# A hybrid decoder layer on one core: its tasks listed in another order, with engines and PSUM banks of copies and splits chosen anew

## The chip, the cores and the metric

One Trainium2 chip, of which one core is used. The time of an execution is the device time in microseconds (us). The number to predict is the median over runs of the changed kernel; that of the kernel before is 780.19 us (three runs: 783.53, 779.92 and 780.19).

## The reference

One decoder layer for 512 positions and 1024 channels in float32, batch 1. The core of it:

```python
mod = (silu(c) @ w_ada + b_ada)
sh1, sc1, gt1, sh2, sc2, gt2 = split(mod, 6)
h = rmsnorm(x, norm1_g) * (1 + sc1) + sh1
z = h @ w_in
zq, zkc, zvc, zks, zvs, zkw, zvw, zg, zs = split(z, cuts)
o_attn = nsa_attention(zq, zkc, zvc, zks, zvs, zkw, zvw, sigmoid(zg), pe_k, pe_v, w_ck1, w_ck2, w_cv1, w_cv2)
y_ssm = s5_mixer(zs, lam_re, lam_im, log_step, b_re, b_im, c_re, c_im, d_skip, w_glu, b_glu)
mix = concat([rmsnorm(o_attn, attn_norm_g), rmsnorm(y_ssm, ssm_norm_g)])
x = x + gt1 * (mix @ w_o)
h = rmsnorm(x, norm2_g) * (1 + sc2) + sh2
u = causal_dwconv(h @ w_up, conv_w, conv_b)
a, v = split(u, 2)
x = x + gt2 * ((silu(a) * v) @ w_down)
return rmsnorm(x, normf_g)
```

`nsa_attention` has 8 query heads and 2 key/value heads of 64, rotary positions on queries and keys, and three branches (compressed blocks of 32 keys, selected blocks, a window), each head's branches mixed by gates. `s5_mixer` is a diagonal state space model with 32 groups of 16 channels and 64 complex states, followed by GELU and a GLU.

## The kernel before, in words

**Matmuls.** Every large product is made of three float32 matmuls at the rounded precision fp32r: `split` (L107 to L109) makes of a float32 operand a high part (a cast, by `cpy`, L64 on ACT, L67 on DVE, L71 on POOL) and a low part (what the cast left over, a subtraction, L109, on DVE or POOL), and `mm3` (L119 to L123) adds high x high (L121), high x low (L122) and low x high (L123). `weights` (L111 to L117) does that for a weight tile: DMA from SP into one of four buffers tagged "raw", then cast and subtraction into one of four buffers tagged "unit". A tile is named by what it is for: `uinq0` to `uinq3` are the four tiles of the query columns of `w_in`, `uos0` to `uos3` and `uoa0` to `uoa3` those of `w_o` for the SSM half and the attention half, `uup` and `udn` those of the feed-forward loop; the raw buffer has `r` in place of `u`.

**Stages.** The first 120 us load x and the state space parameters, make the modulation from `w_ada`, the normalised and transposed h (`hh`, `hl`), the tables of the state space model, and the projections of keys and values. To 160 us POOL and DVE run the scan of the state X (`madd`, L689 to L692: a product pra, a sum ada, an addition to X), while PE computes the hidden layer of the compressed keys (hid, L747). `comp` takes that hidden layer through a GELU (copy to cg L67, then `gelu2`, L1242 to L1247, ACT and DVE in turn), transposes it (hT, L759) and multiplies it on (co, L763 and L772). Then the four query tiles zq0 to zq3 are projected, each over eight k-tiles, two of them in each of uinq0 to uinq3, and each is rotated by `rope` (L611 to L613 on DVE, L616) and transposed into QS (qx, L794 to L798). The powers of the model (VV, L348 and L349: two products, of which one lands in a temporary vw, and their sum) are made beside that. From 200 us on, the attention runs by query tile and pair of heads: scores (L834), masked maxima (L839 and L848), exponentials on ACT (L853), scaling by the gates (L64, L69 or L73), transposes p (L895), and products with the values (po, L901). Between them stand the SSM outputs y, their transposes yT (L1036), GELU (ys, ga), split (yh) and GLU (L1057), the sums for the norms (ssq, with `rsqrt` in L171 to L173: DVE, then a power on POOL), and the output projection: `residual` (L1081 to L1092) for the SSM half (os) and for the attention half (oa), where F (L908 on) makes mixa (L919) from the attention output. N0 to N3 normalise for the feed-forward layer (hx, L944 and L947, then a split to h2h and h2l), and eup computes the first columns of it with the two early weights eu. From 400 to 755 us the feed-forward loop runs 22 blocks of up and 22 of down weights, and the end normalises and stores.

**What sets the order.** Two tables in the source. `ORDER` lists 210 task names; each is called once in that order. `PICK` holds choices that differ from a default: for a copy or subtraction its engine (`e_...`, `h_...`: A, V or P), for a tile its PSUM bank group (`ps_...`: acc 3, tr 2, ms 2, pv 1) or its buffer. Both are looked up by `kn`. The calls are not the final order: the tile scheduler arranges the instructions of each engine by its own estimate of when they can start, with the order of the calls as a priority, and puts in the waits. So the table moves instructions also in places that it does not name.

Of the kernel before, what the change touches and what calls it, by code (L numbers as in the profile page):

```python
# [18 lines left out]
ORDER = """  # L19
ident c x0 xn0 x1 xn1 x2 xn2 x3 xn3 rows sp vt silu a0 p0 ws0 step a1 p1 z0 z1 ws1 z2 dT a2 p2 z3 ws2 pw bc a3 p3 z4 z5 ws3 ri bct0 bct1 z6  # L20
z7 Bb1 Bb2 W W1 W0 zu U0 U1 cst A4 X W3 KS mid wk1 wk2 wk0 U2 wk3 s2 L1 U3 wv0 W2 L2 wv2 zk1 L3 L0 g11 kx1 wv3 zk0 kx0 zk3 kx3 Ss b2 zk2 g13
VC wv1 zv1 chain g12 kx2 cw g10 zv0 zv2 VV b1 AM1 b0 AM0 VV3 zv3 hid0 hid1 hid2 hid3 comp wq0 wq3 wq1 wq2 zq0 qx0 zq1 zq3 qx3 zq2 qx2 VV5
qx1 M s3 VV0 s1 VV6 VV2 b3 VV1 K1 s0 S00 O00 XV K2 K0 K3 S01 O01 glu0 glu1 VV4 S02 O02 K4 K5 Y1 K6 Y0 S03 yh O03 VV7 K7 Y2 ys Y3 yT0 S10 yT1
O10 ge0 yT3 ge1 yT2 S11 ge3 ge2 gl3 S12 O11 xr gl1 gl0 gl2 gt1 O12 ssq wos R1 woa S13 O13 S20 O20 S21 O21 S22 O22 S23 S30 O23 R0 R3 R2 F1 F0
O30 S31 O31 S32 S33 O32 O33 cv F2 N0 N1 F3 N2 N3 eu0 eup0 eu1 eup1
# [4 lines left out]
def kn(name, *opts):  # L30
    if opts:
        SEEN.setdefault(name, opts)
    return PICK.get(name, opts[0] if opts else SEEN[name][0])
D = 1024
# [1276 lines left out]
```

## Time and profile before

| | us |
|---|---|
| runs (median of three) | 780.19 (779.92 to 783.53) |
| the profiled execution, its own time | 781.08 |
| its span, first to last instruction | 779.3 |
| PE busy | 713.8 (92% of the span) |
| DVE busy | 476.7 (61%) |
| POOL busy | 315.5 (40%) |
| ACT busy | 298.6 (38%) |
| mean granted TensorE clock | 0.972 |

PE is TensorE's matmuls, DVE VectorE, ACT ScalarE, POOL GpSimd, SP the queue that issues the transfers. A busy engine may be busy beside another one; only where PE waits does the work of the others show in the time.

### The profile page before, as it was taken

The page shows a single profiled execution, that of the slowest core. Times are in us where ns is not written, and L with a number is a line of the kernel's source. Part 1 is how long each engine was busy: PE and PEld are TensorE (multiplying, and loading weights), DVE is VectorE, ACT ScalarE, POOL GpSimd, SP SyncE. Part 2 cuts the span into 40 slices and gives each one's busy share as a digit, 9 for nine tenths or more (in the row PEclk, how much of TensorE's full clock was granted, in tenths as well). Part 3 has the DMA queues.
Part 4 walks back from the last instruction along what each step waited for, and adds up shares of the span by engine and source line. Part 5 has one row for each costly group of instructions (what it writes and reads, how often), then busy time and mean ns, then how long its engine had stood idle before and what let it go on. Part 6 is the DMA issues. An engine that isn't in the chain of part 4 may idle for free.

```text
span 779.3 us, 11258 instructions
## 1 busy us (share of the span) xinstructions
PE 713.8 (92%) x4171; PEld 570.3 (73%) x4171; DVE 476.7 (61%) x1011; ACT 298.6 (38%) x617; POOL 315.5 (40%) x312
## 2 busy tenths in 40 slices
PE   3998998878799898989889999999999999999993
PEld 2677787546677576768589888888888888888883
DVE  3369848369877786685775477465753554323337
ACT  7444325111476956255423333332333321212223
POOL 2589947897521525254531320310233113131023
PEclk9999999979989999999979999999999999999997
DMA  8666235752121017000052143343422333323102
GB/s 267 235 225 222 95 127 161 276 222 78 30 46 38 1 45 279 2 1 6 22 209 94 61 156 132 111 135 109 142 102 81 109 109 108 109 82 108 55 1 108
DMA packets 30843, 87.64 MB, mean 112 GB/s; under 512 B 4712, under 2 KB 9252, under 8 KB 30757
## 3 DMA queue, kind: packets, MB, share of 16 engines
q1 hardware_dynamic: 30789, 86.92, 32.9%
q8 instruction: 33, 0.54, 0.3%
q14 instruction: 21, 0.17, 0.1%
HBM read 82.71 MB, written 2.10 MB: 109 GB/s over the span
## 4 chain that ended last, share of the span: by engine, by line
PE 72%; DVE 9%; POOL 6%; DMA 6%; ACT 4%; issue 3%; SPq 0%; POOLq 0%; ACTq 0%; DVEq 0%
PE up L123 10%; PE up L121 10%; PE up L122 9%; PE dn L123 5%; PE dn L122 5%; PE dn L121 5%; PE po L901 2%; PE sc L834 2%; PE p L895 2%; DMA raws<-in_bc_dram 2%; POOL prl L689 1%; PE eup L121 1%; PE y L1015 1%; PE eup L122 1%; PE eup L123 1%
## 5 line engine op out<-in xcount | busy, mean ns | idle before, releaser
L123 PE MATMUL up<-h2h,uup 128*128 128x512 f32 x320 | 126.3, 395 | 0.0
L121 PE MATMUL up<-h2h,uup 128*128 128x512 f32 x320 | 126.3, 396 | 0.0
L122 PE MATMUL up<-h2l,uup 128*128 128x512 f32 x320 | 126.0, 394 | 0.0
L1178 DVE SCALAR_TENSOR_TENSOR us<-up,cst,us 128x511 f32<-128x511 f32 x80 | 59.8, 747 | 64.4 <-ACT us L1176 63.2
L1176 ACT ACTIVATE us<-up,cst 128x512 f32<-128x512 f32 x40 | 31.1, 778 | 105.9 <-PE up L123 105.8
L123 PEld LDWEIGHTS up<-h2h,uup 128*128 128x128 f32 x320 | 60.1, 188 | 14.2
L122 PEld LDWEIGHTS up<-h2l,uup 128*128 128x128 f32 x320 | 60.0, 188 | 14.1
L121 PEld LDWEIGHTS up<-h2h,uup 128*128 128x128 f32 x320 | 60.1, 188 | 13.9
L122 PE MATMUL dn<-udn,ghs 128*128 128x512 f32 x176 | 68.5, 389 | 0.0
L123 PE MATMUL dn<-udn,ghs 128*128 128x512 f32 x176 | 68.5, 389 | 0.0
L121 PE MATMUL dn<-udn,ghs 128*128 128x512 f32 x176 | 68.0, 389 | 0.0
L109 POOL TENSOR_TENSOR uup<-rup,uup 128x1024 fp32r<-128x1024 f32 x13 | 32.8, 2525 | 64.7 <-ACT uup L64 51.4
L109 DVE TENSOR_TENSOR uup<-rup,uup 128x1024 fp32r<-128x1024 f32 x27 | 37.1, 1375 | 14.8 <-ACT uup L64 14.7
L73 POOL TENSOR_SCALAR Ss<-Ss,sm 128x384 f32<-128x384 f32 (+3 forms) x38 | 23.2, 622 | 42.0 <-DVE sm L857 24.7
L109 POOL TENSOR_TENSOR udn<-rdn,udn 128x1024 fp32r<-128x1024 f32 x7 | 17.2, 2458 | 54.7 <-DVE udn L67 27.2
L121 PEld LDWEIGHTS dn<-udn,ghs 128*128 128x128 f32 x176 | 33.0, 188 | 6.9
L122 PEld LDWEIGHTS dn<-udn,ghs 128*128 128x128 f32 x176 | 33.0, 188 | 6.9
L123 PEld LDWEIGHTS dn<-udn,ghs 128*128 128x128 f32 x176 | 33.0, 188 | 6.8
L834 PE MATMUL sc<-KS,QS 128*128 128x288 f32 (+2 forms) x128 | 32.6, 355 | 3.5 <-DVE mp L848 1.7
L853 ACT ACTIVATE Ss<-Ss,mx 128x128 f32<-128x128 f32 (+3 forms) x64 | 35.1, 550 | 0.0
L64 ACT ACTIVATE uup<-rup 128x1024 fp32r<-128x1024 f32 x28 | 29.4, 1050 | 12.7 <-PE up L123 12.7
L109 DVE TENSOR_TENSOR udn<-rdn,udn 128x1024 fp32r<-128x1024 f32 x15 | 19.9, 1328 | 17.1 <-ACT udn L64 10.4
(450 smaller groups left out, 1729.6 us busy)
## 6 DMA issues: line engine op xcount, KB each, us to landing
rup<-in_w_up_dram SPq DMA_DIRECT2D x44, 512.0 KB, 3.4
rdn<-in_w_down_dram SPq DMA_DIRECT2D x22, 512.0 KB, 3.2
mid<-in_w_ada_dram SPq DMA_DIRECT2D x14, 512.0 KB, 4.0
adaa<-in_w_ada_dram SPq DMA_DIRECT2D x8, 512.0 KB, 6.1
adap<-in_w_ada_dram SPq DMA_DIRECT2D x8, 512.0 KB, 5.4
adag<-in_w_ada_dram SPq DMA_DIRECT2D x8, 512.0 KB
adab<-in_w_ada_dram SPq DMA_DIRECT2D x7, 512.0 KB, 3.5
xt<-in_x_dram SPq DMA_DIRECT2D x4, 512.0 KB, 5.4
```

The lines of the kernel that those rows point to most:

```text
L64: A.activation(dst, src, AF.Copy, **({} if s is None else {"scale": s}))
L73: P.tensor_scalar(dst, src, s, 1.0, op0=ALU.mult, op1=ALU.mult)
L109: eng.tensor_tensor(out=lo, in0=src, in1=f(hi), op=ALU.subtract)
L121: PE.matmul(ps, w[0], m[0], start=start, stop=False)
L122: PE.matmul(ps, w[0], m[1], start=False, stop=False)
L123: PE.matmul(ps, w[1], m[0], start=False, stop=stop)
L834: PE.matmul(ps[:, :n], v.QS[:, h, qs], v.KS[:, g, x, c0:c0 + n], start=x == 0, stop=x == 1)
L853: A.activation(Sv[:, br, :nk], Sv[:, br, :nk], AF.Exp, bias=mx[:, e, 1 + br:2 + br], scale=0.125, accum_out=sm[:, e, 1 + br:2 + br])
L895: PE.transpose(pc_[:, o:o + 128], v.Ss[:, ui, e, br, kc * 128:(kc + 1) * 128], ident)
L901: PE.matmul(half(e), VT[:, kc, br, g], pT[:, o:o + 128], start=kc == 0 and br == 0, stop=kc == qt > 0 and br == 1)
L1176: A.activation(u_, ps, AF.Identity, bias=cv[:, 3, c_:c_ + 1], scale=cv[:, 2, c_:c_ + 1])
L1178: V.scalar_tensor_tensor(u_[:, d:], ps[:, :S - d], cv[:, 2 - d, c_:c_ + 1], u_[:, d:], op0=ALU.mult, op1=ALU.add)
```

## The change

Only the two tables are edited; the 210 tasks, the 3519 matmuls and the arithmetic are the same. In `PICK` some 65 entries are added, dropped or changed: engines of about 50 copies and splits, the PSUM bank group of nine tiles, two buffers (mixa2 from raw to pt, pz101 to sw). Those that the prediction speaks of, one entry to a line:

```diff
-'h_inv3': 'V'
+'h_inv3': 'P'
...
+'e_os1': 'V'
...
-'h_oa3': 'V'
...
-'e_h23': 'V'
```

`e_os1` is the engine of the subtraction for uos1 (default POOL); `h_oa3` that of the cast for uoa3 (default ACT); `e_h23` that of the low part of the last tile of h2 (default POOL); `h_inv3` that of the cast of a tile of the value columns. About twenty of the other entries are casts and subtractions of uup, udn and gh in the feed-forward loop, of which most change between DVE and POOL, in both directions.

In `ORDER` about forty names stand elsewhere. Two of its lines, where the places below are:

```diff
-VC wv1 zv1 chain g12 kx2 cw g10 zv0 zv2 VV b1 AM1 b0 AM0 VV3 zv3 hid0 hid1 hid2 hid3 comp wq0 wq3 wq1 wq2 zq0 qx0 zq1 zq3 qx3 zq2 qx2 VV5
...
+g13 wv1 zv1 chain g12 kx2 cw g10 zv0 VV zv2 zv3 AM1 b1 b0 VV3 AM0 hid0 hid1 hid2 hid3 VC comp wq0 wq3 wq2 wq1 zq0 qx0 zq1 zq3 qx3 VV5 zq2
```

**First place: compressed keys and query weights (about 158 to 180 us).** On DVE, the GELU of the compressed keys among the scan's additions and the casts of the query weights. Before:

```order
L691 TENSOR_TENSOR ada3_1210<-pra3_1209 128x224
L692 TENSOR_TENSOR X_714<-X_714,ada3_1210 128x7x32
L67 COPY cg_1463<-hid_1414 128x256
L1244 TENSOR_SCALAR cg_1463<-cg_1463 128x256
L689 TENSOR_TENSOR pra5_1219<-A4_685,zu_661 128x448
L1245 TENSOR_TENSOR cg_1463<-cg_1463 128x256
L691 TENSOR_TENSOR ada5_1220<-pra5_1219 128x224
L692 TENSOR_TENSOR X_714<-X_714,ada5_1220 128x7x32
L67 CAST uinq0_1492<-rinq0_1490 128x1024
L1247 SCALAR_TENSOR_TENSOR cg_1463<-cg_1463 128x256
```

Now:

```order
L689 TENSOR_TENSOR pra3_1208<-A4_686,zu_622 128x448
L691 TENSOR_TENSOR ada3_1209<-pra3_1208 128x224
L67 COPY cg_1463<-hid_1413 128x256
L692 TENSOR_TENSOR X_715<-X_715,ada3_1209 128x7x32
L1244 TENSOR_SCALAR cg_1463<-cg_1463 128x256
L1245 TENSOR_TENSOR cg_1463<-cg_1463 128x256
L689 TENSOR_TENSOR pra5_1218<-A4_686,zu_622 128x448
L691 TENSOR_TENSOR ada5_1219<-pra5_1218 128x224
L1247 SCALAR_TENSOR_TENSOR cg_1463<-cg_1463 128x256
L67 CAST uinq0_1492<-rinq0_1490 128x1024
L692 TENSOR_TENSOR X_715<-X_715,ada5_1219 128x7x32
```

The last step of the GELU (L1247) stands ahead of the cast of uinq0 and of the second addition to X; the copy to cg stands ahead of the first. On POOL, the low halves of the four query weights among the last steps of the scan. Before:

```order
L109 TENSOR_TENSOR uinq0_1492<-rinq0_1490,uinq0_1492 128x1024
L691 TENSOR_TENSOR ada6_1225<-pra6_1224 128x224
L689 TENSOR_TENSOR pra7_1229<-A4_685,zu_661 128x448
L109 TENSOR_TENSOR uinq3_1497<-rinq3_1495,uinq3_1497 128x1024
L109 TENSOR_TENSOR uinq1_1502<-rinq1_1500,uinq1_1502 128x1024
L692 TENSOR_TENSOR X_714<-X_714,ada6_1225 128x7x32
L691 TENSOR_TENSOR ada7_1230<-pra7_1229 128x224
L109 TENSOR_TENSOR uinq2_1507<-rinq2_1505,uinq2_1507 128x1024
L692 TENSOR_TENSOR X_714<-X_714,ada7_1230 128x7x32
```

Now:

```order
L109 TENSOR_TENSOR uinq0_1492<-rinq0_1490,uinq0_1492 128x1024
L691 TENSOR_TENSOR ada6_1224<-pra6_1223 128x224
L689 TENSOR_TENSOR pra7_1228<-A4_686,zu_622 128x448
L109 TENSOR_TENSOR uinq3_1497<-rinq3_1495,uinq3_1497 128x1024
L109 TENSOR_TENSOR uinq2_1502<-rinq2_1500,uinq2_1502 128x1024
L692 TENSOR_TENSOR X_715<-X_715,ada6_1224 128x7x32
L109 TENSOR_TENSOR uinq1_1507<-rinq1_1505,uinq1_1507 128x1024
L691 TENSOR_TENSOR ada7_1229<-pra7_1228 128x224
L692 TENSOR_TENSOR X_715<-X_715,ada7_1229 128x7x32
```

uinq2 and uinq1 have changed places, and the sum ada7 is now behind the subtraction of uinq1. On PE the first three query tiles now use uinq0 one after the other, and all that is left of them needs uinq1 first. Further on, on DVE, one of the sums VV that stood ahead of the first rotary instruction (L611 of zq0) is behind it.

**Second place: the GLU among the scores (about 268 to 280 us).** On PE, the first matmuls of the GLU (their operands are the four tiles of yh) and the scores sc of the last units of query tile 2. Before:

```order
L834 MATMUL sc261_3055<-KS_736,QS_1510 128x512
L887 MATMUL pc201_2929<-ident_67,scz1_104 128x128
L895 MATMUL p2010_2933<-ident_67,Ss_1026 128x128
L834 MATMUL sc261_3055<-KS_736,QS_1510 128x512
L895 MATMUL p2010_2933<-ident_67,Ss_1026 128x128 x2
L834 MATMUL sc270_3065<-KS_736,QS_1510 128x288
L895 MATMUL p2010_2933<-ident_67,Ss_1026 128x128
L121 MATMUL glu3_2453<-yh_2184,uglu0_1983 128x512
L121 MATMUL glu1_2545<-yh_2184,uglu0_1983 128x512
L834 MATMUL sc270_3065<-KS_736,QS_1510 128x288
L122 MATMUL glu3_2453<-yh_2184,uglu0_1983 128x512
```

Now:

```order
L834 MATMUL sc250_2948<-KS_553,QS_1510 128x288 x2
L121 MATMUL glu0_2453<-yh_2184,uglu0_1972 128x512
L121 MATMUL glu3_2471<-yh_2184,uglu0_1972 128x512
L895 MATMUL p2002_2876<-ident_67,Ss_904 128x128 x4
L122 MATMUL glu0_2453<-yh_2184,uglu0_1972 128x512
L123 MATMUL glu0_2453<-yh_2184,uglu0_1972 128x512
L122 MATMUL glu3_2471<-yh_2184,uglu0_1972 128x512
L123 MATMUL glu3_2471<-yh_2184,uglu0_1972 128x512
L887 MATMUL pc200_2849<-ident_67,scz0_103 128x128
L834 MATMUL sc251_2954<-KS_553,QS_1510 128x512 x2
L834 MATMUL sc260_3049<-KS_553,QS_1510 128x288 x2
L834 MATMUL sc261_3055<-KS_553,QS_1510 128x512 x2
```

GLU tiles 0 and 3 begin ahead of sc251 to sc270; before, tiles 3 and 1 began behind sc251, sc260 and sc261 and among sc270. On DVE the first subtraction for yh is the 430th row of the engine instead of the 461st. sc271 and the scores of tile 3, which stood among the GLU matmuls, now stand behind most of them.

**Third place: the weights of the SSM half (about 300 to 310 us).** On POOL, the powers r_s of the norm and the subtractions of uos. Before:

```order
L173 TENSOR_TENSOR r_s_108<-vs0_2648,mh_70 128x1
L173 TENSOR_TENSOR r_s_108<-vs1_2652,mh_70 128x1
L73 TENSOR_SCALAR Ss_1026<-Ss_1026,sm300_3089 128x512
L173 TENSOR_TENSOR r_s_108<-vs2_2656,mh_70 128x1
L109 TENSOR_TENSOR uos1_2670<-ros1_2668,uos1_2670 128x1024
L173 TENSOR_TENSOR r_s_108<-vs3_2660,mh_70 128x1
L109 TENSOR_TENSOR uos2_2675<-ros2_2673,uos2_2675 128x1024
L1092 TENSOR_TENSOR xr_2540<-xr_2540,ots10_2696 128x512
```

Now:

```order
L173 TENSOR_TENSOR r_s_108<-vs0_2621,mh_70 128x1
L173 TENSOR_TENSOR r_s_108<-vs1_2625,mh_70 128x1
L173 TENSOR_TENSOR r_s_108<-vs2_2629,mh_70 128x1
L109 TENSOR_TENSOR uos2_2648<-ros2_2646,uos2_2648 128x1024
L73 TENSOR_SCALAR Ss_904<-Ss_904,sm211_3047 128x384 x2
L173 TENSOR_TENSOR r_s_108<-vs3_2633,mh_70 128x1
L73 TENSOR_SCALAR Ss_904<-Ss_904,sm300_3089 128x512
L1092 TENSOR_TENSOR xr_2607<-xr_2607,ots10_2669 128x512
```

uos1 has left POOL for DVE, where it stands between uos0 and uos3; uos2 stays and comes behind the third power instead of behind the fourth; scalings of scores have come in behind it.

## Rows read from the trace of the kernel before

**Rows 1.** Windows by stretch: stretch, length, busy us (instructions) of each engine, PEclk, DMA share, GB/s.

```profile
160.00:199.00 39.00, 31.13 (x141) 24.05 (x142) 31.51 (x34) 7.09 (x11) 33.01 (x23) 0.82 0.30 111
...
260.00:314.00 54.00, 47.37 (x337) 36.66 (x337) 41.57 (x152) 36.10 (x88) 26.62 (x27) 1.00 0.32 118
...
400.00:755.00 355.00, 355.00 (x1612) 293.75 (x1611) 182.89 (x223) 102.35 (x131) 77.08 (x41) 1.00 0.30 103
```

**Rows 2.** The same view, one stretch of 5 us.

```profile
165.00:170.00 5.00, 4.53 (x26) 3.60 (x26) 3.42 (x3) 1.97 (x5) 5.00 (x4) 0.50 0.30 107
```

**Rows 3.** Waits of PE: what waited <- releaser: us in total, times, longest us.

```profile
PE eup L121 <- ACT eu L64: 4.5, 1, 4.5
PE q L794 <- DVE QS L798: 3.9, 4, 2.3
PE hT L759 <- DVE cg L1247: 3.7, 1, 3.7
PE zq L121 <- DVE rope L613: 3.5, 1, 3.5
...
PE sc L834 <- DVE mp L848: 1.7, 2, 1.4
PE os L122 <- POOL uos L109: 1.7, 1, 1.7
...
PE oa L123 <- DVE mixa L919: 1.4, 1, 1.4
PE glu L122 <- DVE yh L109: 1.4, 1, 1.4
```

**Rows 4.** Timeline of DVE, 162 to 165 us: start, duration, instruction.

```profile
162.32 1.20 DVE L692 TENSOR_TENSOR X<-X,ada 128x224 f32<-128x224 f32 x1
163.44 0.68 DVE L67 CAST uinq<-rinq 128x1024 fp32r<-128x1024 f32 x1
164.04 0.41 DVE L1247 SCALAR_TENSOR_TENSOR cg<-cg 128x256 f32<-128x256 f32 x1
```

**Rows 5.** Timeline of PE, 168 to 170 us.

```profile
168.73 0.63 PE L123 MATMUL zq<-uinq,hl 128*128 128x512 f32 x1
169.16 0.63 PE L121 MATMUL zq<-uinq,hh 128*128 128x512 f32 x1
```

**Rows 6.** Timeline of POOL, 171 to 179 us.

```profile
171.57 2.39 POOL L109 TENSOR_TENSOR uinq<-rinq,uinq 128x1024 fp32r<-128x1024 f32 x1
...
175.16 2.85 POOL L109 TENSOR_TENSOR uinq<-rinq,uinq 128x1024 fp32r<-128x1024 f32 x1
```

**Rows 7.** Timeline of DVE, 174 to 192 us.

```profile
174.62 3.94 DVE L348 TENSOR_TENSOR vw<-RI,C 128x512 f32<-128x512 f32 x2 [6.20 <-POOL X L692]
...
180.16 0.68 DVE L348 TENSOR_TENSOR vw<-RI,C 128x512 f32<-128x512 f32 x1
...
189.41 1.28 DVE L349 TENSOR_TENSOR VV<-VV,vw 128x512 f32<-128x512 f32 x2
...
191.54 0.41 DVE L613 TENSOR_TENSOR rope<-zq,cst 128x256 f32<-128x256 f32 x1
```

**Rows 8.** Timelines of POOL (first two rows) and DVE, 302 to 309 us.

```profile
302.36 2.39 POOL L109 TENSOR_TENSOR uos<-ros,uos 128x1024 fp32r<-128x1024 f32 x1
...
306.21 2.34 POOL L109 TENSOR_TENSOR uos<-ros,uos 128x1024 fp32r<-128x1024 f32 x1
...
303.81 2.02 DVE L109 TENSOR_TENSOR uos<-ros,uos 128x1024 fp32r<-128x1024 f32 x1 [1.59 <-ACT uos L64]
```

**Rows 9.** Timeline of DVE, 333 to 336 us.

```profile
333.63 2.11 DVE L67 CAST uoa<-roa 128x1024 fp32r<-128x1024 f32 x1 [0.69 <-PE os L123]
```

**Rows 10.** Timeline of DVE, 392 to 394 us.

```profile
392.01 1.21 DVE L109 TENSOR_TENSOR eu<-rup,eu 128x1024 fp32r<-128x1024 f32 x1
```

**Rows 11.** The page's part 5, two groups: group, count, busy us, mean ns, idle before.

```profile
L73 POOL TENSOR_SCALAR Ss<-Ss,sm 128x384 f32<-128x384 f32 (+3 forms) x38 | 23.2, 622 | 42.0 <-DVE sm L857 24.7
...
L853 ACT ACTIVATE Ss<-Ss,mx 128x128 f32<-128x128 f32 (+3 forms) x64 | 35.1, 550 | 0.0
```

More of the change, by code (lines that the diff above doesn't have):

```diff
@@ L19 @@
 ORDER = """
-ident c x0 xn0 x1 xn1 x2 xn2 x3 xn3 rows sp vt silu a0 p0 ws0 step a1 p1 z0 z1 ws1 z2 dT a2 p2 z3 ws2 pw bc a3 p3 z4 z5 ws3 ri bct0 bct1 z6
-z7 Bb1 Bb2 W W1 W0 zu U0 U1 cst A4 X W3 KS mid wk1 wk2 wk0 U2 wk3 s2 L1 U3 wv0 W2 L2 wv2 zk1 L3 L0 g11 kx1 wv3 zk0 kx0 zk3 kx3 Ss b2 zk2 g13
-VC wv1 zv1 chain g12 kx2 cw g10 zv0 zv2 VV b1 AM1 b0 AM0 VV3 zv3 hid0 hid1 hid2 hid3 comp wq0 wq3 wq1 wq2 zq0 qx0 zq1 zq3 qx3 zq2 qx2 VV5
-qx1 M s3 VV0 s1 VV6 VV2 b3 VV1 K1 s0 S00 O00 XV K2 K0 K3 S01 O01 glu0 glu1 VV4 S02 O02 K4 K5 Y1 K6 Y0 S03 yh O03 VV7 K7 Y2 ys Y3 yT0 S10 yT1
@@ L24 @@
-O10 ge0 yT3 ge1 yT2 S11 ge3 ge2 gl3 S12 O11 xr gl1 gl0 gl2 gt1 O12 ssq wos R1 woa S13 O13 S20 O20 S21 O21 S22 O22 S23 S30 O23 R0 R3 R2 F1 F0
-O30 S31 O31 S32 S33 O32 O33 cv F2 N0 N1 F3 N2 N3 eu0 eup0 eu1 eup1
+c x0 ident xn0 x1 xn1 x3 x2 xn2 rows sp xn3 silu vt a0 p0 ws0 step a1 p1 z0 z1 ws1 z2 dT a2 p2 z3 ws2 pw bc a3 p3 z4 z5 ri ws3 z6 KS bct0
+Bb1 bct1 W Bb2 z7 zu W1 W0 U1 U0 cst A4 X W3 mid wk1 wk2 U2 wk0 wk3 s2 L1 U3 wv0 wv3 W2 L2 wv2 zk1 L3 L0 Ss g11 kx1 zk0 kx0 zk3 kx3 b2 zk2
+g13 wv1 zv1 chain g12 kx2 cw g10 zv0 VV zv2 zv3 AM1 b1 b0 VV3 AM0 hid0 hid1 hid2 hid3 VC comp wq0 wq3 wq2 wq1 zq0 qx0 zq1 zq3 qx3 VV5 zq2
@@ L26 @@
+qx1 s3 VV0 s1 VV6 VV2 b3 M qx2 XV VV1 glu1 K1 s0 S00 O00 K2 K0 K3 S01 glu0 O01 S02 VV4 O02 K4 K5 K6 Y1 Y0 S03 yh O03 VV7 K7 ys Y3 Y2 yT0 S10
+O10 yT1 ge0 yT3 ge1 yT2 S11 ge3 ge2 gl0 gl3 S12 O11 gl1 gl2 gt1 xr ssq wos R1 woa S13 O12 S20 O13 O20 S21 S22 O21 O22 S23 S30 O23 S31 R0 R3
+R2 F1 F0 O30 S32 O31 S33 O32 O33 cv F2 N0 N1 F3 N2 N3 eu0 eup0 eu1 eup1
 """
```

2 lines of the change are left out of this document (1 added, 1 removed).

## The prediction

> **What bounds the kernel now.** Read the busy time by stretch first. From 400 to 755 us TensorE is busy for all of the 355 us at full clock [rows 1]: the feed-forward loop is a run of matmuls with no hole, so nothing that other engines do there can shorten it, only break it. Ahead of it there are holes: in 160 to 199 us PE is busy 31.1 of 39, in 260 to 314 us 47.4 of 54. The change touches an engine's order, so what it is worth is the part of these holes that it closes. Next come the waits of PE, which name each hole by the instruction that ended it [rows 3]: the compressed keys' transpose hT waits 3.7 us for the GELU on DVE, the query projection zq 3.5 us for a rotary instruction on DVE (it holds the PSUM bank that zq wants), two query transposes q and others 3.9 us for QS, GLU 1.4 us for yh, a score 1.4 us for the masked maxima, the SSM half of the output projection (os) 1.7 us for a split on POOL, its attention half (oa) 1.4 us for mixa, and the early FFN columns (eup) 4.5 us for a weight that is late. A hole can cost more than its length: behind the 3.7 us one, 165 to 170 us ran at a granted clock of 0.50 [rows 2], which is 1.2 GHz of 2.4, and the 512-column matmuls follow each other 0.43 us apart [rows 5], half of that at full clock.
>
> The set of matmuls is the same before and after, so the sum is one of waits. It is made against the profiled execution: 781.08 us, which is 0.89 above the median of 780.19. In the first 160 us PE keeps nearly its old order and waits for transfers, which come in an order of which only neighbours are exchanged: 0.
>
> **Compressed keys and queries (160 to 199 us).** DVE now does the GELU's last step, L1247, ahead of one addition to the SSM state (X, 1.20 us) and of the cast of uinq0 (0.60 us from its start to that of L1247) [rows 4]. hT can thus start 1.20 + 0.60 = 1.8 us sooner, and zq some 2 us sooner, at about 166 instead of 168. But the four weight tiles are taken in another order. Tasks zq0, zq1, zq3 first use uinq0 alone: 3 tasks x 2 k-tiles x 3 matmuls = 18, at 0.43 us 7.7 us, so to about 173.7. Then comes uinq1. Its low half ended at 171.57 + 2.39 = 174.0 on POOL; it is now behind that of uinq2 and X, in the place that ended at 175.16 + 2.85 = 178.0 [rows 6], less the addition (some 0.6) that has gone behind it: 177.4. PE has three hi x hi products of uinq1 and one modulation sum (10 short matmuls) to fill in, about 2 us; so it stands still for some 1.5 to 2 us, and what hT gained is gone. It is not lost either, because the next hole takes it up: from 177.4 PE has 72 - 18 - 3 = 51 matmuls until zq2, 11 us at full clock (0.22 each) and up to 2 more if the clock falls, so it is there at 188.6 to 190.6, and the bank that zq2 needs comes free with the third rotary instruction, at 191.54 + 0.41 = 191.95 now [rows 7]. Ahead of that, DVE has one sum VV less: of the two in 189.41 + 1.28 one goes behind, **-0.6 us**. What DVE does in this run is stretched by POOL: two products vw took 3.94 us together, beside a subtraction on POOL that took 2.85, and one product alone 0.68 [rows 6, 7]. Both bounds are from there: if the new order takes the two apart, 3.94 - 2 x 0.68 = 2.6 more is won, so -3.2. On the other side, uinq1's low half may be pushed by two such products, 3.9 us, to 181.3; the 51 matmuls, begun at half clock, then end at 181.3 + 11 + 2 = 194.3 or a little later, +2.9 against 192.
>
> **GELU and GLU (260 to 285 us).** The first low half of yh is the 430th instruction of DVE instead of the 461st, and PE begins with GLU tiles 0 and 3, ahead of the last scores of query tile 2 which it did first before. The wait of 1.4 us for yh should go: **-1.4 us**. The wait for the maxima (1.4 us, the same stage) is at least moved; I count it as staying. Bounds: both go, -2.8; or the scores, now later, are late for what follows them, up to +9.4 (the slower rival, below).
>
> **Output projection, SSM half (300 to 314 us).** POOL did two subtractions for this weight, uos1 (from 302.36) and uos2 (from 306.21, 2.34 us) with a power between them, and PE waited 1.7 us for the second [rows 3, 8]. POOL keeps uos2 alone; uos1 goes to DVE, which had done uos0 and idled 1.59 us before uos3 [rows 8]. uos2 then starts when its cast is there, some 2.3 us sooner, and the wait of 1.7 us has cover: **-1.7 us**. Bounds: -1.7, since no more is there; +0.6 if DVE comes late (below).
>
> **Attention half (314 to 345 us).** The cast of uoa3 goes from DVE, where it took 2.11 us beside POOL's splits [rows 9], to ACT, and the last attention units are laid between the SSM tiles and the first attention tile. mixa, on DVE behind that cast, comes up to 2.1 us sooner, more than the 1.4 us of its wait: **-1.4 us**; bounds -1.4 and +1.1 (the shift is lost, and the low half of uoa2 on DVE is stretched from the 1.21 us of such a subtraction by itself to POOL's 2.34 [rows 8, 10]).
>
> **The rest.** Before eup one of seven small instructions on DVE is moved behind the split that frees the raw slot; the weight must still be fetched after it: 0, at most a few tenths. In the feed-forward loop some 20 splits and casts change engine. PE's unbroken 355 us cover them, and 0 it is; without that cover each subtraction moved to POOL would cost 2.34 - 1.21 = 1.1 us, by the rows of the two engines [rows 8, 10]. In the wait for QS only the order of the transposes is changed, a hole of 3.9 us with no cause removed: 0, bounds -2.3 and +2.3 (its longest wait).
>
> **Sum.** -0.6 - 1.4 - 1.7 - 1.4 = -5.1, so 781.08 - 5.1 = 776.0 for the profiled run and, less 0.89, **775.1 us** against the median. Its own range, with terms half won or with one of the -2.6 kind added, is 772.5 to 778.
>
> **Rivals.**
>
> *Larger.* The hole at 192 us shrinks by the whole 3.2 us, both waits of the GELU stage go, and the half clock after the holes gets shorter too (a 5 us stretch at 0.50 is 2.5 us of lost clock [rows 2]): -3.2 - 2.8 - 1.7 - 1.4 = -9.1, that is 771.1. For it: all of these are waits for DVE or POOL, of which the change shifts each. Against it: the query stage has a new wait, for uinq1.
>
> *No gain.* The engines' work is the same in amount, and a wait that closes reopens one task on: hT's 1.8 us show this already. If each of the four holes returns three quarters of its gain, -1.3 is left: 779, and no measurement of this kernel tells less than 0.5% (3.9 us) from no change.
>
> *Slower.* The scores that GLU now goes ahead of decide. A unit of scores passes DVE (maxima), ACT (four exponentials at 0.55 us, 2.2) and POOL or ACT (four scalings at 0.62, 2.5) [rows 11] before PE can transpose it: 4.7 us at least. Before, the last unit of query tile 2 and the first of tile 3 had their scores ahead of or among the 48 GLU matmuls, and that chain ran beneath these (11 us at 0.22 each). Now the GLU matmuls are mostly done when the scores come. If PE comes to the transposes of a unit less than 4.7 us after its scores, it stands for the rest; if both units lose their cover whole, that is 2 x 4.7 = 9.4 us, and the sum is 9.4 - 5.1 = +4.3, or 784.5. For it: ACT and DVE are busy 36 and 42 of 54 us here [rows 1], so the chain seldom runs without a queue. Against it: the SSM half's projection, 96 matmuls, follows, and the order lays it between those scores and their transposes in part.
>
> *One engine shuts out the other.* The subtraction of uos3 on DVE started at 303.81, while POOL's of uos1 ran until 304.75, and ended 1.08 us later, at 305.83; one that ran by itself took 1.21 [rows 8, 10]. It did next to nothing until POOL was done. The Trainium skill ("SBUF — State Buffer", section "Who interferes with whom") says the same of a VectorE instruction with two SBUF inputs beside a GpSimd one: the second to issue is fully blocked until the first ends, and the order of issue alone decides. The trace agrees here, with the 2.02 us. For the change this cuts both ways: if POOL's subtraction of uos2 starts first, that of uos1 on DVE comes 2.34 us late, PE waits for uos1 in place of uos2, and the place costs 2.34 - 1.7 = +0.6 instead of -1.7. The sum is then -2.8, and the time 777.4. Against it: ACT casts uos1 before uos2, so DVE should be first.
>
> **How the numbers follow.** Forecast 0.50, larger 0.15, no gain 0.13, slower 0.17, shut out 0.05. Faster by over 0.5% means under 776.3. The forecast's range lies about seven parts in ten below it: 0.35, with the larger gain 0.50. Slower: 0.17. The rest, 0.33, is the same. The range reaches from 770, below the larger case, to 783, which leaves out most of the slower case and the tail of the larger one, some 2 in 10 together.
>
> **What would show it.** Right: hT's wait falls under 2 us and a new wait of zq for uinq on POOL of 1 to 2.5 us appears; the wait for the rotary instruction falls below 3 us and ends near 191; no wait of os for POOL, none of oa for mixa over 0.5 us; GLU's wait for yh gone; 355 us of loop still without a hole. Wrong: a wait of zq for uinq over 4 us; new waits of p for scaled scores over 4 us in 270 to 305 us; or PE waits before 400 us that add up to no less than now.

## The result, and the profile of the kernel after

The changed kernel takes 785.33 us (median of 20 runs, 781.14 to 793.87) where the kernel before takes 780.97 us in the same session (20 runs, 778.36 to 784.09). The ratio is 1.0057, 95% interval 1.0037 to 1.0077: **slower by 0.6%**, 10 us above the forecast and outside its range. One run of the change, 793.87 us, over 1.5% above its fastest, is left out of the ratio. The profiled execution took 784.95 us, with a span of 783.2 us and a mean granted clock of 0.963 (before: 781.08, 779.3, 0.972). Two counts given ahead of the prediction are off: the tables `PICK` differ in 57 entries, not some 65, and the profiles of both kernels have 4171 matmuls on PE, where 3519 were named.

Part 1 of its page, to be read beside the table of the kernel before:

```profile
PE 718.1 (92%) x4171; PEld 571.9 (73%) x4171; DVE 469.3 (60%) x1008; ACT 298.5 (38%) x616; POOL 323.4 (41%) x316
```

DVE is busy 7 us less, POOL 8 us more; PE, with the same matmuls, is busy 4.3 us longer. Now the waits of PE (what waited <- releaser: us in total, times, longest):

```profile
PE q L794 <- DVE QS L798: 4.1, 4, 2.4
PE eup L121 <- ACT eu L64: 3.8, 1, 3.8
...
PE sc L834 <- DVE mp L848: 2.1, 1, 2.1
PE h L942 <- ACT hx L947: 1.9, 3, 1.1
PE hT L759 <- DVE cg L1247: 1.7, 1, 1.7
...
PE pc L887 <- DVE scz L858: 1.3, 1, 1.3
...
PE zq L121 <- DVE KS L767: 1.3, 1, 1.3
PE zq L121 <- DVE rope L613: 1.3, 1, 1.3
PE p L895 <- DVE pt L67: 1.2, 1, 1.2
```

Against [rows 3] the waits that the forecast named did shrink: hT from 3.7 to 1.7, zq for the rotary instruction from 3.5 to 1.3; those of GLU for yh (1.4), of os for POOL (1.7) and of oa for mixa (1.4) are gone. In their places stand others: zq for KS, pc for scz and p for pt with 1.2 to 1.3 us each, a longer one of sc for mp (2.1), and more of h for hx. And yet the time went up. The windows of the same stretches (columns as in [rows 1], and 200 to 345 us added):

```profile
160.00:199.00 39.00, 32.29 (x167) 22.77 (x164) 30.33 (x36) 6.11 (x11) 32.57 (x22) 0.84 0.43 155
260.00:314.00 54.00, 49.15 (x340) 37.01 (x339) 46.17 (x161) 38.12 (x94) 23.58 (x26) 0.97 0.33 118
200.00:345.00 145.00, 133.47 (x1140) 101.72 (x1140) 110.34 (x476) 91.44 (x271) 55.06 (x61) 0.96 0.20 59
400.00:755.00 355.00, 355.00 (x1614) 294.26 (x1613) 179.13 (x219) 101.49 (x130) 87.75 (x47) 1.00 0.31 106
```

The kernel before, same view:

```profile
200.00:345.00 145.00, 130.85 (x1136) 99.69 (x1134) 110.03 (x477) 90.46 (x273) 55.82 (x62) 0.98 0.20 59
```

The loop is unbroken as before. In 260 to 314 us PE is busy 49.15 us instead of 47.37, so there is less waiting, but the granted clock there has fallen from 1.00 to 0.97; in 200 to 345 us the two figures are 133.47 against 130.85 us, and 0.96 against 0.98. TensorE waits less and takes longer for the same work. The experiments ask why.

### The profile page after: what moved, and what is told of

Read it like the earlier page. It is cut to its first block, busy times and chain, and to the rows that moved or that the text cites. A ratio compares the mean times of both kernels' runs of the same rounds, so it can differ in the third digit from the quotient of the medians.

```text
span 783.2 us, 11254 instructions
## 1 busy us (share of the span) xinstructions
PE 718.1 (92%) x4171; PEld 571.9 (73%) x4171; DVE 469.3 (60%) x1008; ACT 298.5 (38%) x616; POOL 323.4 (41%) x316
## 5 line engine op out<-in xcount | busy, mean ns | idle before, releaser
L109 POOL TENSOR_TENSOR uup<-rup,uup 128x1024 fp32r<-128x1024 f32 x12 | 29.6, 2462 | 92.4 <-ACT uup L64 82.0
L109 DVE TENSOR_TENSOR uup<-rup,uup 128x1024 fp32r<-128x1024 f32 x28 | 38.8, 1385 | 16.4 <-ACT uup L64 16.3
L109 POOL TENSOR_TENSOR udn<-rdn,udn 128x1024 fp32r<-128x1024 f32 x10 | 25.0, 2496 | 20.6 <-ACT udn L64 15.9
L901 PE MATMUL po<-pt,VT 128*64 128x128 f32 x320 | 28.4, 298 | 0.3 <-ACT pt L64 0.3
```

The lines of the kernel that those rows point to most:

```text
L109: eng.tensor_tensor(out=lo, in0=src, in1=f(hi), op=ALU.subtract)
L901: PE.matmul(half(e), VT[:, kc, br, g], pT[:, o:o + 128], start=kc == 0 and br == 0, stop=kc == qt > 0 and br == 1)
```

## The experiments

**The same kernels again** (no edit: a second profiled execution of each, so that what one execution does by chance can be told from what the change does).

> The kernel before once more, unchanged, for a second profile. It says which shifts between two profiles of one kernel are chance: below 0.5 us at every mark if the marks can be trusted, up to 2 us if transfers at the start and the granted clock vary.

> The changed kernel once more, unchanged, for a second profile. In the first one TensorE's start was 0.87 us late against before (first transpose 10.38 for 9.51 us), the first state matmul 1.65, the first L 3.98, the first query product 2.79, the end 3.90. If the start and the half clock at 35 to 45 us are this kernel's own, all of these come again within 0.5 us; if they are of that execution, the first transpose is back at 9.2 to 9.7 us and the shift at L is 1 to 2 us, and the loss must be somewhere else.

Measured: 782.13 and 784.23 us. The loop's first matmul (up) starts at 424.0 (before: 423.0) and at 426.2 us (after: 426.9); from there to the end of the last matmul (dn) each takes 344.3 us. So all of the difference arises ahead of the loop. In the first profile of after the tasks to 120 us ran up to 4 us late; in the second the first transpose was still late (10.04 us, against 9.25 in before_again), but the first L (96.75 against 97.14) was not, the hidden layer came 0.8 us sooner than in the first profile of before and hT 1.5 us sooner. The lateness of the front was chance, and the gain in hT was there.

**Front or back.** front_undone is the change with the first 103 tasks listed as before and the eight front choices as before; front_alone is the kernel before with these edits alone.

```diff
-c x0 ident xn0 x1 xn1 x3 x2 xn2 rows sp ...
+ident c x0 xn0 x1 xn1 x2 xn2 x3 xn3 rows sp ...
...
-'e_We30': 'V', 'e_rowg11': 'V', 'h_hh1': 'P', 'h_inv3': 'P', 'ps_ky2': 'ms'
+'e_U000': 'V', 'e_U110': 'V', 'e_U111': 'A', 'h_inv3': 'V'
```

> The changed kernel with the first 103 tasks (to comp, some 165 us) in the order of the kernel before, and with the eight choices of engine and bank that belong to them undone; the rest is the change. Theory front: all of the loss (3.8 us on TensorE by 119 us, 3.9 at the end) is made ahead of 120 us, so this comes to 780 to 782 (ratio 0.998 to 1.001), or lower if the rest of the change gains. Theory back: the order of attention, GLU and output projection loses by itself, what the front loses would be taken up by later waits, so this stays at 784 to 786 (1.004 to 1.006). Theory scatter: any other order shifts everything by some us either way, and the four runs of this call do not add up.

> The kernel before with the first 103 tasks in the order of the change and the eight choices that belong to them; the rest is as before. Theory front: 784 to 786 (ratio 1.004 to 1.006), with the first query, key and state matmuls some 3 us later than before. Theory back: 780 to 782. If this and the run with the front undone add up to the change (ratios less 1 sum to 0.0057), the two halves are independent.

Measured: 785.74 us, 1.0051 (1.0027 to 1.0074), and 788.34 us, 1.0108 (1.0065 to 1.0151). The front by itself loses 1.1%, the back by itself 0.5%, both together 0.6%. The parts don't add up, as the theory of scatter had it; the likely reason, not shown by itself, is that every edit changes the scheduler's estimates for all that follows.

**The first 15 tasks.** x_alone is the kernel before with these in the order of the change, x_undone the change with these as before.

```diff
-ident c x0 xn0 x1 xn1 x2 xn2 x3 xn3 rows sp vt silu
+c x0 ident xn0 x1 xn1 x3 x2 xn2 rows sp xn3 silu vt
```

> The kernel before with only its first 15 tasks in the order of the change: ident after c and the first tile of x, x3 ahead of x2, xn3 behind sp, vt behind silu. Theory front, start: the first tiles of x land later, the first transpose starts 0.9 us later, and that is carried to the end and grows: 782 to 784. Theory front, later part: the start moves, but the loss at 30 to 120 us is from other moves: 781 to 782, and the 30 to 60 us look as before.

> The changed kernel with only its first 15 tasks back in the order of the kernel before. Theory front, start: the first transpose is back at 9.5 us, the half clock at 35 to 45 us goes, and the time falls by 2 to 4 us to 781 to 783. Theory front, later part: 0.9 us less at most, 784 to 785.

Measured: 782.46 us, 1.0000 (0.9984 to 1.0016), and 802.65 us, 1.0251 (1.0225 to 1.0278). Fifteen tasks at the start that by themselves are worth nothing are worth 2% once the choices are those of the change; no theory on record had that. In x_undone the largest new wait of PE is far from them, in the tables of the state space model:

```profile
PE K L985 <- DVE VV L349: 9.5, 1, 9.5
```

**List or choices.** order_alone has the change's `ORDER` and the `PICK` of before; pick_alone the reverse.

```diff
-PICK = {... of the change ...}
+PICK = {... of before ...}
```

> The list of task names of the change with the choices of engines and banks of the kernel before. Theory order: the loss is of the order, 784 to 786 (ratio 1.004 to 1.006). Theory choices: the moves of splits and copies between engines lose, so this is 780 to 782. Theory scatter: slower than the change, as any list and any choices that were not made for each other.

> The choices of engines and banks of the change with the list of the kernel before. Theory order: 780 to 782. Theory choices: 784 to 786. Theory scatter: slower than both, since the choices were made for another list.

Measured: 781.87 us, 1.0003 (0.9974 to 1.0033), and 826.53 us, 1.0579 (1.0547 to 1.0611). The list alone changes nothing that can be measured; the choices without their list are a disaster: waits of PE add up to 80.4 us in the whole span, against 52.5 in the change. The loss of the change appears only when its choices are there.

**Groups of choices undone in the change.** fpick_undone takes back the eight front choices, bank_undone six banks and buffers, att_undone eleven choices of engines in attention and output projection, ffn_undone 32 of the feed-forward loop.

```diff
 fpick_undone: the eight entries above
 bank_undone:
-'ps_K6': 'tr', 'ps_y1': 'acc', 'ps_sc320': 'ms', 'ps_sc331': 'ms', 'mixa2': 'pt', 'pz101': 'sw'
 att_undone:
-'e_os1': 'V', 'e_oa11': 'V', 'e_pT2111': 'A', 'e_sm10110': 'V', 'e_sm31001': 'V', 'e_sy0': 'V'
+'e_h23': 'V', 'h_oa3': 'V', 'e_sy2': 'V', 'e_sm01100': 'V'
-'e_sm21111': 'V'
+'e_sm21111': 'P'
 ffn_undone:
-'h_up31': 'V', 'e_dn16': 'P', 'ps_up12': 'ms', ...
+'h_up21': 'V', 'e_dn0': 'P', 'e_gh6': 'P', ...
```

> The list of the change, and its choices but for the eight of the first 165 us (engines of copies of U and We, of rowg11, of the casts hh1 and uinv3, the bank of ky2), which are as before. The list alone took the time of the kernel before, so the loss of some 4 us is in the choices; this run and the next three undo one group each of the 57. Theory front choices: 781 to 782. Else 784 to 786.

> The change with six choices of place undone: the PSUM bank groups of K6, y1, sc320 and sc331, and the buffers of mixa2 and pz101. In both profiles of the change the SSM outputs y begin at 210 us instead of 227, ahead of the first softmax chain, and the loss appears between the last query product and the first transposes of probabilities and again between 290 and 390 us. Theory banks: y1 in the bank group of the scores and query tiles lets it start early and takes a bank from them: 781 to 782. Else 784 to 786.

> The change with eleven choices of engine of the attention, the norms and the output projection undone (scalings of scores, one copy of a transposed tile, the sums for the second norm, uos1 back to POOL, uoa3's cast back to DVE, the last split of h2 back to DVE). By the prediction these moves gain 1.7 + 1.4 us, so 787 to 788; theory engines: they are what loses, 781 to 782.

> The change with the 32 choices of the feed-forward loop undone (splits of up and down weights, gates, four banks). TensorE has no wait there before or after, so by every theory this stays at 784 to 786; 781 to 782 would say that they act on the time where no wait shows.

Measured: 1.0042 (1.0023 to 1.0060), 1.0031 (1.0011 to 1.0051), 1.0079 (1.0048 to 1.0109) and 1.0039 (1.0020 to 1.0058). None gives the loss back, and none can be told from 1.0057 by itself. In ffn_undone the loop takes the same 344.3 us, so those choices are hidden, as forecast. att_undone leans to the slow side, with a median of 788.85 us where the prediction's terms gave 787 to 788: these are the choices that close the waits of os and oa.

**One bank: ps_y1.** With it PE begins the outputs y at 210 us instead of 227 and spreads them over more time among the scores and transposes.

```diff
-'ps_y1': 'acc'
```

> The changed kernel with one choice undone: the PSUM bank of y tile 1 (ps_y1), which lets PE begin the SSM outputs y near 210 us instead of 227 and so mixes them longer among scores, transposes and products with the values. In the traces y and the products with the values (po) take 1.0 and 1.3 us more in the changed kernel than before for the same matmuls. Theory A (the mixing costs that): some 1.5 us less than the changed kernel, ratio 1.003 to 1.004. Theory B (the time goes with the granted clock and with where each execution loses it): 1.005 to 1.006, no different from the change.

Measured: 785.21 us, 1.0044 (1.0025 to 1.0063), between the two theories. The trace is clearer than the time: added up from start to next start, less the waits, the y matmuls occupied PE 9.5 us before, 10.3 to 10.7 in the change, and 9.7 with this choice undone. It costs some 0.8 us, which the kernel's time by itself cannot tell. But the mixing that theory A blamed is not the reason: y stands in 21 unbroken pieces before, in 18 in the change, and in 24 with the choice undone. Why y takes longer stays open.

**What a hole costs behind its end.** The three kernels before_fill, after_fill and order_fill put 32 matmuls without effect into the hole of 4.5 us in which PE waits for the early weight ([rows 3], the row of eup), in the kernel before, in the change, and in order_alone.

```diff
+if j == s == 0:
+    for k in range(KO):
+        for e in range(4):
+            PE.matmul(v.early[j, s][:, :256], v.h2[0][:, k, :128], v.h2[0][:, k, :256], start=True, stop=True)
 up(v.early[j, s], v.early_us[j], s, slice(0, 384))
```

> The kernel before, with 32 matmuls of 256 columns more (high x high products of h2, written into the first PSUM tile of eup before its own sum starts there, so nothing of the result changes). They are to run in the hole of 4.5 us in which PE waits for the early FFN weight; behind that hole the profile before shows half clock from about 391.8 to 397.9 us, which costs some 3 us. Theory (what a hole costs behind its end counts in full, and this kernel loses time to it): the hole's length stays, eup's first matmuls follow each other 0.16 us apart instead of 0.32, the mean granted clock rises by some 0.003 to 0.004, the time falls by 3 us, ratio 0.996 (0.995 to 0.998). Rival (the granted clock is a reading beside the time, or what is given back here is lost again later in the loop): ratio 1.000 plus or minus 0.001.

> The changed kernel with the same 32 filling matmuls ahead of eup. Theory: the loss of clock behind this hole (half clock from 396.0 to some 401 us) is in both kernels alike, so the fill gives 2.5 to 3 us and what separates the two kernels stays: ratio about 1.002 (1.000 to 1.004) to the kernel before. Rival (the changed kernel's lower mean clock comes from holes like this one and its whole loss goes with it): ratio at or below that of the filled kernel before, 0.996. Second rival (nothing is won by a fill): 1.0057.

> The list of tasks of the change, the choices of engines and banks of the kernel before (which by itself was 1.0003), with the same fill. Theory: 0.996 to 0.997, a version faster than both kernels. Rival: 1.000.

Measured: 796.43 us, 1.0193 (1.0172 to 1.0214); 785.12 us, 1.0035 (1.0014 to 1.0056); 798.28 us, 1.0136 (1.0076 to 1.0195). The six runs of order_fill fall into two groups, two at 787 to 788 us and four at 797 to 803, so that its ratio stands for neither. before_fill and order_fill miss every theory: the fill did what it should, eup's first matmuls followed each other 0.17 us apart, and in before_fill the time rose by 14 us in all four runs. The ratio of after_fill lies in the range of its theory, but its interval reaches nearly to the change's own 1.0057, so it shows no gain. In before_fill the timeline of PE and the windows show where the time went (first rows of start, duration, instruction and idle time before it, then windows):

```profile
415.04 0.66 PE L121 MATMUL eup<-h2h,eu 128*128 128x128 f32 x4 [2.70 <-ACT h2h L64]
416.48 0.47 PE L122 MATMUL eup<-h2l,eu 128*128 128x128 f32 x1 [0.79 <-DVE h2l L109]
...
435.96 0.41 PE L123 MATMUL eup<-h2h,eu 128*128 128x128 f32 x1
436.17 0.73 PE L121 MATMUL up<-h2h,uup 128*128 128x512 f32 x1
```

```profile
410.00:415.00 5.00, 2.34 (x14) 2.02 (x12) 2.86 (x5) 2.00 (x2) 0.00 (x0) 1.00 0.88 318
415.00:420.00 5.00, 4.18 (x21) 4.04 (x21) 1.43 (x2) 0.00 (x0) 0.00 (x0) 0.61 0.49 170
420.00:425.00 5.00, 5.00 (x25) 5.00 (x25) 1.50 (x2) 0.78 (x1) 0.00 (x0) 0.50 0.00 0
...
435.00:440.00 5.00, 5.00 (x16) 4.23 (x16) 1.50 (x2) 1.30 (x2) 1.10 (x1) 0.50 0.02 3
440.00:445.00 5.00, 5.00 (x23) 4.04 (x23) 1.51 (x3) 0.78 (x1) 0.17 (x1) 1.00 0.00 0
```

The scheduler, which counts the fill as work, had moved a cast that waits for a transfer (uup, 412.98 us) ahead of the high half of h2's last tile on ACT. PE stood still for 2.7 us, and then ran the 128-column matmuls of eup at a granted clock of 0.50, 0.21 us each, without a pause for 19.7 us. The clock came back only after the 512-column matmuls of up had begun. A hole of 3.5 us in all cost four times its length.

How much such a hole costs is not fixed. The profiled execution of after_fill took 799.76 us where its ten others took 781.74 to 786.82, and there a hole of 1.3 us ahead of the same short matmuls was enough: they began at full clock, lost it at 423.7 us, and did not get it back until the 512-column matmuls of up had begun (timeline, then windows).

```profile
421.70 0.33 PE L122 MATMUL eup<-h2l,eu 128*128 128x128 f32 x1 [1.32 <-POOL h2l L109]
...
439.59 0.73 PE L121 MATMUL up<-h2h,uup 128*128 128x512 f32 x1
```

```profile
420.00:425.00 5.00, 3.68 (x28) 3.54 (x28) 0.00 (x0) 0.00 (x0) 1.65 (x1) 0.87 0.32 120
425.00:430.00 5.00, 5.00 (x26) 5.00 (x25) 1.50 (x2) 0.78 (x1) 0.00 (x0) 0.50 0.00 0
...
440.00:445.00 5.00, 5.00 (x15) 3.86 (x14) 3.31 (x5) 1.13 (x2) 0.00 (x0) 0.58 0.02 3
```

In the profiled execution of order_fill, 787.91 us, the short matmuls had no hole just ahead of them and ran at full clock.

**The same fill without that hole.** fill_cast moves the cast of one early weight from ACT to POOL, which also puts the cast of uup behind the high half of h2; fill16_cast has 16 filling matmuls instead of 32.

```diff
+'h_up10': 'P'
```

> before_fill with one engine changed: the cast of the early weight of block 1 goes from ACT to POOL. In before_fill that cast stood on ACT ahead of the high half of the last tile of h2 and kept it waiting for the weight's transfer; PE then stood still for 2.7 us ahead of the 128-column matmuls of eup and ran these at half clock, 415 to 436 us. Theory (the 14 us of before_fill are the clock behind that hole, lost because the matmuls that follow it are short ones): without the hole the 128-column matmuls run at 0.11 us each as in the kernel before and the time falls from 796.4 to 783 to 785, ratio 1.001 to 1.004 (the fill itself ran at half clock and delayed eup by 2.5 us, about what the full clock gives back). Rival (filling itself, a longer unbroken run of PE, brings the half clock on): ratio about 1.019 again, with 20 us at half clock and no hole ahead of them.

> The same with 16 filling matmuls instead of 32, so that at 0.185 us each (what they took in before_fill) they end at about 391.5 us and do not delay eup, which in the kernel before starts at 391.8. Theory: eup starts on time, is at full clock from about 393.5 instead of 397.9, and 2 us are won: ratio 0.997 (0.996 to 0.999). Rival (the clock is lost again elsewhere): 1.000 or more.

Measured: 781.77 us, 0.9992 (0.9971 to 1.0014), and 781.65 us, 0.9993 (0.9971 to 1.0015). fill_cast has the same fill, no wait at 412 to 416 us, and its short matmuls run at full clock, 0.11 us apart (its windows, same columns, and its first rows there):

```profile
410.00:415.00 5.00, 5.00 (x37) 5.00 (x37) 2.36 (x2) 1.55 (x2) 0.00 (x0) 1.00 0.82 304
415.00:420.00 5.00, 5.00 (x47) 5.00 (x47) 2.01 (x3) 2.08 (x3) 0.00 (x0) 1.00 0.13 53
```

```profile
412.95 0.56 PE L121 MATMUL eup<-h2h,eu 128*128 128x128 f32 x4
413.34 0.27 PE L122 MATMUL eup<-h2l,eu 128*128 128x128 f32 x1
413.45 0.27 PE L123 MATMUL eup<-h2h,eu 128*128 128x128 f32 x1
```

So it was the hole and what followed it, not the filling, that cost 14 us; the ratio lies even below the 1.001 to 1.004 expected. The 2 us hoped for from fill16_cast did not come. In its profile the fill started at 392.32 and eup at 396.2 us, with the clock at 0.80 in 395 to 400 us; a gain under 0.3% would not show in its interval. No version beats the kernel before by what can be measured.

## Why the prediction was wrong

**The waits were nearly right.** From one profile of each kernel, the waits of PE by stage, as means over the six kernels that have the list and the choices of before but for the first 15 tasks, the fill and its cast (before, before_again, x_alone, before_fill, fill_cast, fill16_cast) and over the seven that have the list of the change (after, after_again, ffn_undone, bank_undone, fpick_undone, att_undone, y1_undone). Lost clock is the sum, over windows of 5 us, of the time that PE is busy x (1 - granted clock); it is an estimate, since within a window it does not tell busy time at full clock from busy time at half.

```
stretch, us    waits: before  change   forecast    lost clock: before  change
160 to 200             9.0     7.6     -0.6                    5.1     4.7
200 to 260             5.0     5.2      0                      2.8     4.3
260 to 300             3.8     3.2     -1.4                    0.4     1.5
300 to 345             4.6     2.5     -3.1                    0.05    0.5
```

In 345 to 385 us the waits are 0 and 0.8 us (3.2 in att_undone, whose profiled execution, 793.43 us, is the slowest of the seven, and at most 0.7 in the others), and in 385 to 410 us, without the filled kernels, 5.9 and 6.2 us. The four terms were forecast at -5.1 us and came to -4.1 (-1.4, -0.6, -2.1). In the query stage zq's wait for the rotary instruction fell by 2.0 to 2.2 us, more than the 0.6 forecast, and hT's by 2.0 in the first pair of profiles and 1.0 in the second, for 1.8 forecast; the wait of zq for uinq on POOL, put at 1.5 to 2 us, was 0.5 us in the first profile, though one for KS of 1.3 us came that was not foreseen. (The upper bound there, +2.9 us, is by its own numbers 194.3 - 191.95, 2.4 us or a little more; nothing rests on it.) GLU's wait went, but the scores' wait for the maxima grew from 1.4 to 2.1 us: the term took one of these for the whole. The waits of os and oa, 3.1 us, went, and with them 1.0 us of sc for mx; 1.3 us (pc for scz) and 1.2 us (p for pt) came.

**The step that failed** is the sentence "The set of matmuls is the same before and after, so the sum is one of waits." The matmuls are the same, but not what they take. Over the first three profiles of each kind (before, before_again, x_alone; after, after_again, ffn_undone), PE's waits from its first matmul up to the loop fell by 3.7 us (44.5 to 40.8) and the time the matmuls occupy it rose by 5.7 us (370.1 to 375.8); with a first matmul 0.6 us later that is the 2.5 us by which the loop starts later in these profiles. The rise has two parts:

- *The clock, 2 to 3 us.* In 200 to 345 us each of the six kernels of the first kind lost 2.7 to 4.2 us of clock, each of the seven of the second 4.3 to 10.0, on average 3.3 against 6.4 (over the first three of each, 2.9 against 4.9). (The mixed kernels stand apart: order_alone 9.0, front_alone 5.4, and front_undone 3.8, which lost 8.2 in 30 to 60 us instead.) Beyond 225 us the waits there are less in sum but not shorter: the longest is 2.13 us (1.8 to 3.0 in the variants with single groups undone) where before it was 1.70. What a hole costs differs between executions. The same hole at the same place, in two executions of the changed kernel, after (timeline, then the window behind it):

```profile
272.23 1.13 PE L834 MATMUL sc<-KS,QS 128*128 128x512 f32 x4 [2.13 <-DVE mp L848]
...
274.95 1.12 PE L901 MATMUL po<-pt,VT 128*64 128x128 f32 x8
...
275.00:280.00 5.00, 5.00 (x37) 4.37 (x37) 4.90 (x17) 3.11 (x12) 2.98 (x4) 0.68 0.00 0
```

and after_again:

```profile
271.48 1.13 PE L834 MATMUL sc<-KS,QS 128*128 128x512 f32 x4 [2.13 <-DVE mp L848]
...
274.16 0.66 PE L901 MATMUL po<-pt,VT 128*64 128x128 f32 x8
...
275.00:280.00 5.00, 5.00 (x37) 4.11 (x34) 4.90 (x18) 3.09 (x13) 3.42 (x4) 1.00 0.00 0
```

  Eight products po took 1.12 us in the one, at a granted clock of 0.68 in 275 to 280 us, and 0.66 in the other, at 1.00. Of the seven profiles six show a stretch at half clock between 268 and 279 us, of the six of the first kind two (266 to 271 us). The mean granted clock is 0.9593 for the change (19 runs) and 0.9644 to 0.9667 for the kernel before (by session). Within the change's own runs the time falls by 4.6 us for each 0.01 of clock, within those of the kernel before by 1.6 to 3.6, so an estimate from these of what goes with the lower clock is 1 to 3 us of the 4.4, wherever in the span it falls. That PE meets more half clock in this stretch is shown; that it comes from particular holes is argued from the rows above and from before_fill.
- *Some groups of matmuls, most of them short ones, some 3 us.* Over the same three profiles of each kind K, U, zv, y, pc, h, yT and cv each take 0.1 to 1.0 us more in the change, 3.8 us together, of which only 0.1 is at half clock; zk, ky and ssqa take 0.2 us less each, which leaves some 3. Three of them follow single choices: y falls from 10.5 to 9.7 us without ps_y1, U and zv return to 1.6 and 13.8 us without the front choices. K, zv, h and yT stand in one or two pieces more among other matmuls than before, but U, pc and cv in as many and y in fewer, so that this is not the reason for all of them, and what is stays open. Each is below what the kernel's time can tell, and their sum hardly above it.

order_alone fits: its waits are 3 us shorter (41.4), it loses 9.0 us of clock in 200 to 345 us, its h, U, zv and y take nearly what they took before (its K, pc and yT are those of the change), and its time is that of the kernel before. By this one profile, the list of tasks won its waits and gave them back in clock, and the choices added h, U, zv and y. The sum -4.1 + 3.1 + 3 gives +2 of the 4.4 us; waits in the first 160 us were 1.0 us more in the change, less than they differ between executions. This remainder stays open, and so does how much of the clock's part belongs to the change for good: one profile of a kernel shows one draw of it.

**The other terms.** The loop at 0: right, 344.3 us in each profile. The front at 0: right for its waits within 1 us, but front_alone, 1.1% slower, shows that it is not an edit without effect: its waits to 160 us are 26.3 us, within the spread, and its lost clock is 6.7 us in 160 to 200 and 2.5 in 260 to 300, where its list and choices are those of before. QS at 0: right (3.9 and 4.1 us). eup at "at most a few tenths": right, 5.9 to 6.2 us with the transposes ahead of it.

**The rivals.** The slower rival's time, 784.5, is the one that came, but not by its mechanism: no wait of p for scaled scores of 0.4 us or more appeared; the nearest is that of pc for scz, 1.3 us, and it has another cause. The shut-out did not hit the instruction that the rival named: the subtraction of uos1 on DVE started at 302.71, ahead of POOL's of uos2 at 303.52, and took 1.23 us, POOL's 2.66 instead of 2.34. The rule of the Trainium skill ("SBUF — State Buffer", section "Who interferes with whom") has it that the one to issue first runs undisturbed; these two numbers agree. But it hit the next instruction of DVE, a product on 128x3 elements (L850), which took 2.36 us instead of the 0.17 us of another one just before, until POOL was done; scz came behind it, and pc waited 1.3 us for that (timelines of after, DVE and then POOL):

```profile
302.57 0.17 DVE L850 TENSOR_SCALAR mx<-mx 128x3 f32<-128x3 f32 x1
...
302.71 1.23 DVE L109 TENSOR_TENSOR uos<-ros,uos 128x1024 fp32r<-128x1024 f32 x1
303.85 2.36 DVE L850 TENSOR_SCALAR mx<-mx 128x3 f32<-128x3 f32 x1
306.12 0.21 DVE L858 TENSOR_TENSOR scz<-scz,sm 128x64 f32<-128x64 f32 x1
...
303.52 2.66 POOL L109 TENSOR_TENSOR uos<-ros,uos 128x1024 fp32r<-128x1024 f32 x1 [1.91 <-ACT uos L64]
```

In after_again and ffn_undone it is the same (2.35 us each, and the wait of 1.3); in att_undone two such instructions took 2.32 us each, and pc waited 3.0 us; in bank_undone, y1_undone and fpick_undone the subtraction of uos2 on POOL runs elsewhere and pc has no such wait. So of the 1.7 us of os's wait that the third term won, 1.3 came back through a shut-out, as far as these timelines tell. A rival that was missing from the list: the waits close much as forecast and the matmuls themselves get dearer. That the clock's part comes from holes that moved to where short matmuls follow them is likely, not shown. The prediction read the cost of the half clock from its rows [rows 2] and put it into one bound of its first term and into the gain of one rival, but nowhere into a loss of its sum.

## What to carry to other kernels

Price a hole by its length and by what runs behind it: ahead of long matmuls 4.5 us of waiting cost some 3 us more, ahead of short ones 3.5 us cost 11 us more, and in one execution of another kernel a hole of 1.3 us was followed by 20 us at half clock. Whether fewer but longer holes are the worse bargain no run here separates. A sum of waits is not a forecast of time where the engine that waits has two speeds: read the granted clock of the stretch that a hole moves into. And where a scheduler turns tables into an order, an edit is not a local one: compare the whole order, and take the parts of a change as good only together with the others.

## What the hardware showed that was not expected

In before_fill TensorE ran 128-column matmuls back to back, with no pause from 416.5 to 436.2 us, and the granted clock stayed at 0.50 through all of it. The 384-column matmuls of the same tile came back to 1.00 within some 6 us at the same place in the kernel before (391.8 to 397.9 us); the same 128-column matmuls, begun at 1.00 with no hole ahead of them, kept it to their end in fill_cast, and, begun at 1.00 behind a hole of 1.3 us, lost it 2 us later in the profiled execution of after_fill and did not get it back before the 512-column matmuls of up. A hole of 2.1 us was followed by a lower clock in one execution and not in the next. And a DVE instruction on 128x3 elements took 2.36 us instead of 0.17 beside a subtraction on POOL.
